# Merging the first transfers, reordering the rest, and moving one more pair of tiles from TensorE to VectorE

## Chip, cores, metric

One core of a Trainium2 chip. The metric is the device time of one execution in microseconds (us), taken as the median of several executions.

## The reference

```python
batch, m, k, n = 16, 512, 1024, 768          # float32 throughout
out = scale * matmul(x, weight) + add_value  # x: (16,512,1024), weight: (1024,768), scale = 0.1
```

The 8192 rows of x are worked off as 64 tiles of 128 rows. The bytes: x 33.55 MB, weight 3.15, add_value 25.17, output 25.17, together 87.03 MB.

## The kernel before

One list is the whole order of the transfers. `x`, `w`, `a` are loads of x tiles, weight chunks and add_value tiles, `o` (and `l`, `r` for the last tile's two pieces) are stores; the numbers are the first tile and how many. All are issued by one queue, in this order. The loop runs tile steps only as far as the next transfer needs them.

```python
STREAM = [
    ("x", 0, 3), ("w", 0, 2), ("w", 2, 2), ("w", 4, 2), ("x", 3, 1), ("w", 6, 2),
    ("a", 0, 3), ("x", 4, 4), ("a", 3, 1), ("x", 8, 4), ("a", 4, 4), ("x", 12, 4),
    ("a", 8, 8), ("x", 16, 8), ("a", 16, 8), ("x", 24, 8), ("a", 24, 8), ("o", 0, 8),
    # ... 20 more, ending in
    ("o", 56, 4), ("o", 60, 1), ("o", 61, 1), ("o", 62, 1), ("l", 63, 1), ("r", 63, 1),
]
X_SLOTS = 16    # tiles of x on the chip at a time
A_SLOTS = 32    # tiles of add_value; the result is written over them and stored from there
PAIRS = [14, 19, 24, 29, 34, 39, 44, 49, 54]   # tiles t, t+1 are turned by VectorE
```

A tile of x is cast to bf16 (GpSimd), turned so that its columns lie on partitions, multiplied, and evicted with scale and add_value (VectorE). Most tiles are turned by TensorE (four transposes into PSUM, then a copy by ScalarE); those in `PAIRS` by VectorE in four quarters, one after each eviction:

```python
def step():
    t = done["step"]
    # ... for the last tile: column pieces instead
    for j in range(KJ):                      # 8 chunks of the contraction
        if j == KJ // 2:
            if t + 1 not in in_pair:
                transpose(t + 1)             # TensorE
            cast_to(min(t + AHEAD, done["x"] - 1))
            if t + 7 in PAIRS:
                cast_pair(t + 7)             # GpSimd
        product(t, j, BOTH)                  # columns 0-511 and 512-767
    finish(t, BOTH[0], 0, N)                 # VectorE: scale, add, write over add_value
    for a in range(P // 32):
        if t + 6 - a in PAIRS:
            turn_pair(t + 6 - a, a)          # VectorE, a quarter of the pair
```

A partition holds eight neighbouring rows of x, add_value and output in memory (`(g p t) k -> p g t k`, t = 8), so an eight-tile x transfer is one 32 KB row for each partition, an add_value or output transfer one of 24 KB. The weight's rows come in runs of two, 6 KB.

## Time and profile before

| | kernel before |
|---|---|
| median time | 210.84 us (210.78 to 210.85, 3 runs) |
| TensorE busy | 196.4 us of a span of 209.2 |
| transfers, packets | 38, 5485 |
| moved | 87.03 MB by the kernel's queue, busy 97.7% |

The profile's busy rows show the share of each of 40 slices in tenths. The chain of waits is followed backwards from the last instruction. A trace also tells when each transfer's completion was counted, sixteen counts for a transfer, one for each DMA engine; "lands" below is the sixteenth, and "spread" is the sixteenth less the first. The lines that carry the reading are in the prediction. One more is needed for comparison, of the timeline of GpSimd: the cast that waits for x tiles 24 to 31.

```profile
73.31 2.03 POOL L109 CAST vx<-xs 128x1024 bf16<-128x1024 f32 x2 [9.08 <-DMA xs<-in_x_dram]
```

Columns: start, busy time, engine and line, what it does, how often, and in brackets the idle time before it and what ended it. These tiles landed at 73.17.

### The profile page before, as it was taken

What the parts mean: (1) busy time and instruction counts of PE and PEld (TensorE: products, weight loads), DVE (VectorE), ACT (ScalarE), POOL (GpSimd) and SP (SyncE); (2) the same over time, 40 slices, a digit from 0 to 9 for tenths busy, and PEclk for the clock granted to TensorE, in tenths of its full rate; (3) what the DMA queues carried; (4) which work ended last, traced back from release to release, by engine and by line L of the source; (5) the groups of instructions that cost most, each with busy time, mean ns of one, the idle gap of its engine ahead of it and who ended that gap; (6) DMA issues with size and microseconds to landing.
All of it is one profiled execution on the core that took longest, in us unless ns stands there. A gap on an engine that the chain in (4) does not pass through costs nothing.

```text
span 209.2 us, 2988 instructions
## 1 busy us (share of the span) xinstructions
PE 196.4 (94%) x1218; PEld 119.5 (57%) x1218; DVE 131.1 (63%) x223; ACT 49.3 (24%) x52; POOL 63.2 (30%) x69
## 2 busy tenths in 40 slices
PE   7599499999999999999999999999999999999990
PEld 2355256656665666566665666565666656666550
DVE  0545413309969969898697886949994994223340
ACT  2513113233103112113032031121130230332310
POOL 1310536420292090503903606303503039100000
PEclk9889979999999999999999999999999999999997
DMA  6999999999999999999999999999999999999993
GB/s 233 418 431 447 423 408 441 451 445 407 404 481 410 418 432 418 432 451 415 437 417 436 436 421 425 442 434 423 423 432 445 445 409 418 432 447 426 409 402 152
DMA packets 5485, 87.21 MB, mean 417 GB/s; under 512 B 608, under 2 KB 736, under 8 KB 2016
## 3 DMA queue, kind: packets, MB, share of 16 engines
q1 hardware_dynamic: 5472, 87.03, 97.7%
q8 instruction: 9, 0.15, 0.3%
q14 instruction: 4, 0.03, 0.0%
HBM read 61.87 MB, written 25.17 MB: 416 GB/s over the span
## 4 chain that ended last, share of the span: by engine, by line
PE 90%; DMA 3%; DVE 2%; ACT 1%; POOL 0%; issue 0%; ACTq 0%; POOLq 0%
PE mm L168 80%; PE tp L146 10%; DMA xs<-in_x_dram 3%; DVE ao L235 1%; ACT xt L152 1%; DVE ao L204 1%; POOL xb L136 0%; DVE xb L132 0%; DVE ao L176 0%; ACTq L152 0%; POOLq L136 0%
## 5 line engine op out<-in xcount | busy, mean ns | idle before, releaser
L168 PE MATMUL mm<-w_bf,xt 128*128 128x512 bf16 (+1 forms) x736 | 130.8, 331 | 0.6 <-DVE ao L204 0.4
L168 PEld LDWEIGHTS <-xt 128*128 128x128 bf16 x736 | 69.6, 99 | 50.8 <-ACT xt L152 11.4
L176 DVE SCALAR_TENSOR_TENSOR ao<-mm,ao 128x768 f32<-128x768 f32 (+2 forms) x62 | 58.3, 944 | 54.1 <-PE mm L168 35.3
L152 ACT COPY xt<-tp 128x1024 bf16<-128x1024 bf16 (+1 forms) x49 | 46.6, 961 | 146.0 <-PE tp L146 146.0
L120 DVE STREAM_TRANSPOSE vt<-vx 32x256 f32<-32x256 f32 x144 | 62.7, 435 | 6.2 <-POOL vx L109 4.0
L136 POOL CAST xb<-xs 128x1024 bf16<-128x1024 f32 x43 | 43.2, 1040 | 56.2 <-DMA xs<-in_x_dram 46.5
L168 PE MATMUL mm<-w_bf,vt 128*128 128x512 bf16 (+1 forms) x288 | 49.7, 326 | 0.0
L168 PEld LDWEIGHTS <-vt 128*128 128x128 bf16 x288 | 28.2, 98 | 17.5
L109 POOL CAST vx<-xs 128x1024 bf16<-128x1024 f32 x18 | 18.3, 1040 | 53.8 <-DVE vt L120 44.7
L146 PE MATMUL tp<-identity,xb 128*128 128x128 f32 x184 | 28.3, 277 | 5.4 <-POOL xb L136 3.0
L146 PEld LDWEIGHTS tp<-identity,xb 128*128 128x128 f32 x184 | 21.7, 143 | 12.1 <-POOL xb L136 3.4
L104 DVE CAST w_bf<-ao 128x768 bf16<-128x768 f32 x8 | 4.1, 557 | 3.8 <-DMA ao<-in_weight_dram 3.8
L132 DVE CAST xb<-xs 128x512 bf16<-128x512 f32 x3 | 1.9, 696 | 5.6 <-DMA xs<-in_x_dram 5.6
L94 PE MATMUL warm<-zeros 128*128 128x512 bf16 x10 | 4.3, 617 | 1.2 <-DVE zeros L82 1.2
L134 POOL CAST xb<-xs 128x512 bf16<-128x512 f32 x2 | 1.6, 834 | 5.5 <-DMA xs<-in_x_dram 5.5
L94 PEld LDWEIGHTS <-zeros 128*128 128x128 bf16 x10 | 1.3, 140 | 3.4 <-issue 2.2
L204 DVE TENSOR_SCALAR ao<-mm 128x768 f32<-128x768 f32 x2 | 1.8, 952 | 2.3 <-PE mm L168 2.3
L235 DVE TENSOR_TENSOR ao<-ao 128x768 f32<-128x768 f32 x3 | 2.7, 950 | 0.0
L134 ACT CAST xb<-xs 128x512 bf16<-128x512 f32 x1 | 0.6, 618 | 4.8 <-DMA xs<-in_x_dram 4.8
L134 ACT ACT_TABLE_LOAD x1 | 1.3, 1283 | 0.7 <-PEq L279 0.7
L201 ACT ACTIVATE ao<-mm 128x768 f32<-128x768 f32 x1 | 0.8, 817 | 0.0
L82 DVE MEMSET zeros<- 128x256 uint32 x1 | 0.3, 272 | 0.9 <-PEq L279 0.9
(6 smaller groups left out, 0.9 us busy)
## 6 DMA issues: line engine op xcount, KB each, us to landing
xs<-in_x_dram SPq DMA_DIRECT2D x6, 4096.0 KB, 27.3
ao<-in_add_value_dram SPq DMA_DIRECT2D x7, 3072.0 KB, 24.3
out_dram<-ao SPq DMA_DIRECT2D x7, 3072.0 KB, 31.2
xs<-in_x_dram SPq DMA_DIRECT2D x3, 2048.0 KB, 22.0
ao<-in_weight_dram SPq DMA_DIRECT2D x4, 768.0 KB, 9.5
xs<-in_x_dram SPq DMA_DIRECT2D x1, 1536.0 KB, 6.0
ao<-in_add_value_dram SPq DMA_DIRECT2D x1, 1536.0 KB, 23.7
out_dram<-ao SPq DMA_DIRECT2D x1, 1536.0 KB, 11.7
```

Of the source, the lines that this page charges most:

```text
L94: nc.tensor.matmul(warm[:, 0:CUT], zeros[:, 0:P], zeros, start=True, stop=True)
L104: nc.vector.tensor_copy(w_bf[:, j + i, :], ao[:, s + i, :])
L109: nc.gpsimd.tensor_copy(vx[:, i, :], xs[:, (t0 + i) % X_SLOTS, :])
L120: nc.vector.transpose(vt[b:b + 32, :, 32 * a:32 * a + 32], pairs[32 * a:32 * a + 32, :, b:b + 32])
L134: other(xb[:, K // 2:K], src[:, K // 2:K])
L136: nc.gpsimd.tensor_copy(xb, src)
L146: nc.tensor.transpose(tp[:, c, :], pairs[:, c * P:(c + 1) * P], identity)
L152: nc.scalar.copy(dst[:, c:c + q, :, :], src[:, c:c + q, :, :])
L168: nc.tensor.matmul(mm_tiles[t, cols[0]][:, n0:n1], lhs(t, j), w_bf[:, j, n0:n1], start=(j == 0), stop=(j == KJ - 1))
L176: nc.vector.scalar_tensor_tensor(a, mm_tiles[t, part][:, n0:n1], float(scale), a, op0=mybir.AluOpType.mult, op1=mybir.AluOpType.add)
L204: nc.vector.tensor_scalar(ao[:, EARLY_AT + t, :], mm_tiles[t, BOTH[0]][:, 0:N], float(scale), None, op0=mybir.AluOpType.mult)
L235: nc.vector.tensor_add(ao[:, t, :], ao[:, EARLY_AT + t, :], ao[:, t, :])
```

## The change

The intent: fewer and longer transfers at the start, where TensorE waits for data; loads and stores in an order that has add_value in time; less work for TensorE, the engine with the highest share.

```diff
 STREAM = [
-    ("x", 0, 3), ("w", 0, 2), ("w", 2, 2), ("w", 4, 2), ("x", 3, 1), ("w", 6, 2),
-    ("a", 0, 3), ("x", 4, 4), ("a", 3, 1), ("x", 8, 4), ("a", 4, 4), ("x", 12, 4),
-    ("a", 8, 8), ("x", 16, 8), ("a", 16, 8), ("x", 24, 8), ("a", 24, 8), ("o", 0, 8),
-    ("x", 32, 8), ("a", 32, 8), ("x", 40, 8), ("o", 8, 8), ("x", 48, 8), ("a", 40, 8),
-    ("o", 16, 8), ("o", 24, 8), ("a", 48, 8), ("x", 56, 8), ("a", 56, 8), ("o", 32, 8),
-    ("o", 40, 8), ("o", 48, 8), ("o", 56, 4), ("o", 60, 1), ("o", 61, 1), ("o", 62, 1),
-    ("l", 63, 1), ("r", 63, 1),
+    ("x", 0, 4), ("w", 0, 4), ("w", 4, 4), ("a", 0, 4), ("x", 4, 4), ("x", 8, 4),
+    ("a", 4, 4), ("x", 12, 4), ("a", 8, 8), ("x", 16, 8), ("a", 16, 8), ("x", 24, 8),
+    ("o", 0, 8), ("a", 24, 8), ("x", 32, 8), ("a", 32, 8), ("x", 40, 8), ("o", 8, 8),
+    ("o", 16, 8), ("a", 40, 8), ("x", 48, 8), ("a", 48, 8), ("x", 56, 8), ("o", 24, 8),
+    ("o", 32, 8), ("a", 56, 8), ("o", 40, 8), ("o", 48, 8), ("o", 56, 4), ("o", 60, 2),
+    ("o", 62, 1), ("l", 63, 1), ("r", 63, 1),
 ]
-PAIRS = [14, 19, 24, 29, 34, 39, 44, 49, 54]
+PAIRS = [14, 19, 24, 29, 34, 39, 44, 49, 54, 59]
-    w_v = weight.rearrange("(c p r) n -> p c r n", p=P, r=2)
+    w_v = weight.rearrange("(c p r) n -> p c (r n)", p=P, r=2)
     # load_w: one transfer now takes n chunks (four), in runs of two rows
+        nc.sync.dma_start(
+            ao[:, s:s + n, :].rearrange("p (c r) n -> p c (r n)", r=2),
+            w_v[:, j // 2:(j + n) // 2, :])
     # [cut: the old load_w, and the head's test for the first x transfer]
```

More of the change, by code (lines that the diff above doesn't have):

```diff
@@ L98, in load_w @@
         s = A_SLOTS - KJ + j
-        if n == 1:
-            nc.sync.dma_start(ao[:, s, :], w_v[:, j // 2, j % 2, :])
-        else:
-            nc.sync.dma_start(ao[:, s:s + 2, :], w_v[:, j // 2, :, :])
+        assert j % 2 == n % 2 == 0
+        nc.sync.dma_start(
+            ao[:, s:s + n, :].rearrange("p (c r) n -> p c (r n)", r=2),
+            w_v[:, j // 2:(j + n) // 2, :])
         for i in range(n):
@@ L249 @@
             done["x"] = s + n
-            if last < EARLY:
+            if s < EARLY:
                 head(op, s, n)
```

## The prediction

> **What bounds the kernel now.** I read the page first, for which engines are full; then the chain of waits, for what the end hangs on; then the timeline of the issuing queue, for which transfer waits for whom; then windows at the end, for who is last.
>
> ```profile
> PE 196.4 (94%) x1218; PEld 119.5 (57%) x1218; DVE 131.1 (63%) x223; ACT 49.3 (24%) x52; POOL 63.2 (30%) x69
> DMA  6999999999999999999999999999999999999993
> q1 hardware_dynamic: 5472, 87.03, 97.7%
> PE 90%; DMA 3%; DVE 2%; ACT 1%; POOL 0%; issue 0%; ACTq 0%; POOLq 0%
> ```
>
> Two resources are full at once. TensorE has 94% and carries 90% of the chain, but the transfers are busy in every slice from the second to the last but one. Stretches of the chain:
>
> ```profile
> 20.67 2.61 DVE ao L235 x3
> 24.36 0.66 PE tp L146 x4
> 25.01 4.28 PE mm L168 x16
> 29.29 0.44 PE tp L146 x4
> 29.73 2.63 PE mm L168 x16
> 203.61 0.42 DVE ao L176
> ```
>
> A tile costs TensorE 2.63 us of products, plus 0.44 if TensorE also turns it. From 24.36 (tile 4's turning) to 203.6 TensorE never stops for more than a fraction. The 4.28 in place of 2.63 is a half-clock stretch (25.8 to 29.2) after an idle of 3.04 us. Before 24.36 it waits for x: tiles 4 to 7 land at 23.21, as the timeline shows by GpSimd's cast:
>
> ```profile
> 6.77 0.33 SPq L254 DMA_DIRECT2D ao<-in_add_value_dram  x1
> 8.61 0.33 SPq L248 DMA_DIRECT2D xs<-in_x_dram  x1
> 23.26 3.99 POOL L136 CAST xb<-xs 128x1024 bf16<-128x1024 f32 x4 [8.52 <-DMA xs<-in_x_dram]
> 138.85 0.96 DVE L176 SCALAR_TENSOR_TENSOR ao<-mm,ao 128x768 f32<-128x768 f32 x1 [3.08 <-DMA ao<-in_add_value_dram]
> 160.82 0.96 DVE L176 SCALAR_TENSOR_TENSOR ao<-mm,ao 128x768 f32<-128x768 f32 x1 [3.06 <-DMA ao<-in_add_value_dram]
> ```
>
> Row one shows that eight transfers can be in flight: the ninth issue comes just after the first landing (6.75). Windows at the end (columns: PE, PEld, DVE, ACT, POOL busy, clock, DMA share, GB/s):
>
> ```profile
> 203.00:204.00 1.00, 0.57 (x6) 0.27 (x3) 0.82 (x2) 0.00 (x0) 0.00 (x0) 1.00 0.96 384
> 204.00:205.00 1.00, 0.00 (x0) 0.00 (x0) 0.04 (x1) 0.00 (x0) 0.00 (x0) 1.00 0.94 373
> 205.00:206.00 1.00, 0.00 (x0) 0.00 (x0) 0.00 (x0) 0.00 (x0) 0.00 (x0) 1.00 0.78 293
> 206.00:207.00 1.00, 0.00 (x0) 0.00 (x0) 0.00 (x0) 0.00 (x0) 0.00 (x0) 0.83 0.26 94
> ```
>
> TensorE and VectorE are done, yet the DMA engines are still 0.94 and 0.78 busy: stores were queued. The trace's completion records say it sharper. The last store was issued at 204.06; the first of the 16 engines finished it at 205.66 (1.6 us, an unqueued store), the slowest at 208.20 (4.1 us). The last tiles' stores, issued at 195.82, 198.89 and 201.96, land at 205.40, 206.31 and 207.24, 0.92 us apart: 0.393 MB at the queue's full rate, not the 3.07 us apart at which TensorE makes tiles. So the end is set by the slowest DMA engine, and TensorE has about 4.1 - 1.6 = 2.5 us of room although the chain names it. The slowest engine is late because each of nine 16 KB instruction loads (every 20 us) takes one engine 1.0 to 1.5 us; the load at 189.9 puts one engine 1.3 us behind all others.
>
> **What the Trainium skill says.** "DMA: Bandwidth & Descriptors", section "Where 436 GB/s comes from", gives 435 GB/s as the ceiling of the fabric; here a 4.19 MB load lands 9.70 us after the one ahead, 432 GB/s, so there is no rate left to gain. Same page, "Queues, rings and completion order": an engine takes its descriptors in ring order. All landings here come in order of issue, so a transfer's landing is told by the bytes issued up to and with it. Same page, "Why a DMA increments its semaphore by 16 and not by 1": only the full 16 says that all has landed; here the 16 spread from 0.3 us early to 2.5 us at the end. "TensorE: Matmul & The Clock Gate", section "What's actually happening": the clock falls to half after an idle window of 3413 ns, windows running free; the trace has two half-clock records of 3.41 us (8.7 to 12.1, 25.8 to 29.2).
>
> **The change part by part.**
>
> Bytes: the same 87.03 MB. Packets of the weight stay 6 KB (the four rows are two runs).
>
> Fewer transfers: 33 for 38. Landing intervals give the fixed cost of one: 0.786 MB of weight take 1.88 us against 0.786 / 0.432 = 1.82; the 0.524 MB tile 1.28 against 1.21. So 0.06 us each, five fewer save 0.3 us of queue time, and this is on the path, since the queue is full to the end.
>
> Head, by bytes and landings of before. x 0-3: 2.10 MB, 6.75 + 0.524/0.42 = 8.0 (was 6.75 for three tiles). First weight half: 3.67 MB, 11.7. Second: 5.24 MB, 15.4. x 4-7 now follow all four add_value rows, 8.91 MB, where before landed 24.18; less about 0.2 for four fewer transfers, 24.0. So tile 4 starts 0.8 us later: TensorE +0.8. The first products move from 10.05 to about 12.3 (11.7 plus a cast of 0.56), but 24 groups of two matmuls at 0.33 us, 7.9 us, end at about 20.5, and tile 3's first half at about 22.4, before tile 4 can begin at 25.1. That delay lies in the existing wait. TensorE's idle before tile 4 is about 2.8 us instead of 3.0: the half-clock window (1.65 us) may come or not.
>
> Pair 59/60: TensorE loses two turnings, 2 x 0.44 = 0.88 us, ScalarE 2 x 1.01. VectorE gains 16 transposes x 0.435 = 7.0 us between 175 and 188, where it is idle 2.1 us of each 3.07. GpSimd's two casts of 1.04 only change target. Net for TensorE: +0.8 - 0.88, about zero; its end stays near 203.6.
>
> Stream order, followed by hand with the landing at a given sum of bytes (63.5 us at 25.17 MB, then 0.432 MB per us). A transfer leaves when its slot is free and those ahead have left. x 24-31 leave at 43.3 (casts of tiles 14, 15), as before. a 32-39 need the first store's landing, 32.51 MB, 80.5 (was 87.8). x 40-47 leave at about 88.7, while the queue is filled to 104.7. a 40-47 need the second store, 50.33 MB, 121.7, filled to 129. x 48-55 follow at 122, filled to 136. a 48-55 leave at 129 (filled to 146), x 56-63 at about 132 (to 153). a 56-63 need store 24-31, 71.30 MB, 170.3, filled to 177.6. So the queue is never empty; the shortest lead is about 7 us.
>
> Who waits for the moved loads: a 40-47 land at 136.3 instead of 138.8 and a 48-55 at 153.3 instead of 160.7, so the two VectorE waits shown go. x 48-55 land at 146.0 instead of 131.4: pair 49 is cast by 149.1 (was 146.6), and its four turnings, each 1.78 with a 0.96 eviction between, end at about 159.4; TensorE wants it at about 160. a 56-63 land at 184.8 instead of 177.7: tile 56's eviction slips from 182.6 to 184.9, and the last quarter of pair 59 ends at 187.7, wanted at about 189. Both fit by 1 us or so, and a slip of up to 2.5 us would not reach the end.
>
> Sum: 0.3 us less of queue, everything else beside it: 210.84 - 0.3 = 210.5 us.
>
> **The rivals.** (a) TensorE is the bound, as its chain says: then later x 4-7 (+0.8), the pair (-0.88) and the clock window (-1.65 to +1.65) decide, 209.1 to 212.4. For it: 90% of the chain. Against: stores landing at the queue's rate after TensorE's end. It can bind only if it loses over 2 us. (b) A late load becomes the wait: x 48-55 or a 56-63 stall pair 49 or 59, some 1 to 2 us of TensorE; with the clock window also lost, the end moves by perhaps 0.5 to 1 us: 211 to 211.5. For it: margins of about 1 us; against: the 2.5 us of room. (c) The lag of the slowest engine changes: the load of instructions at 189.9 falls on another engine, 1.3 us less (209.2), or a second one is hit twice, 1 us more (211.5). Sixteen fewer TensorE instructions among 2436 should not shift the pattern. (d) The head's larger transfers fill the queue sooner (its rate is 86 and 184 GB/s in the second and third us): at most a few tenths, 210.2.
>
> **Range and chances.** 2% is 4.2 us. Faster by that would need the queue to move 87 MB above 440 GB/s; slower, an empty queue of 4 us, which the replay does not find but may have missed in one of its waits. Rival (c) is the widest on both sides. Predicted 210.5 us, range 209.7 to 211.4; faster 0.01, same 0.97, slower 0.02.
>
> **What would show it.** Right: DMA at 9 in all middle slices; last stores landing about 0.9 us apart per tile and more than 3 us after issue on the slowest engine; TensorE's last product within 1.7 us of 203.5; x 4-7 cast at about 24 instead of 23.26; GpSimd waiting for x near 146; VectorE's waits for add_value gone near 138 and 160, a new one near 184.8. Wrong: a slice of the DMA row under 9 in the middle, the last store landing 1.6 to 2 us after its issue (then TensorE was the bound), or TensorE idle before tiles 49 or 59 for over 2 us.

## The result

211.13 us (210.87 to 211.39, 6 runs) against 210.82 (210.56 to 210.93, 6 runs) for the kernel before in the same rounds: ratio 1.0017, 95% interval 1.0004 to 1.003. A ratio is the mean time of one kernel's fast runs over that of the other's of the same rounds, so it is not quite the ratio of the medians. The time is inside the predicted range and within 2%, but on the other side of the kernel before: 0.3 us longer, where 0.3 us less was predicted.

The page after, the rows that answer to those of before:

```profile
PE 195.5 (93%) x1210; PEld 118.4 (57%) x1210; DVE 139.5 (67%) x239; ACT 47.3 (23%) x50; POOL 65.0 (31%) x69
DMA  7999999999999999999999999999999999999993
DMA packets 5021, 87.21 MB, mean 417 GB/s; under 512 B 528, under 2 KB 656, under 8 KB 1552
q1 hardware_dynamic: 5008, 87.03, 97.7%
DMA 58%; PE 21%; DVE 10%; POOL 4%; issue 2%; SPq 2%; POOLq 0%
```

The work of the engines moved as planned: TensorE and ScalarE have less, VectorE 8.4 us more. The transfers are as full as before. Yet the chain of waits, which was 90% TensorE, is now 58% DMA, for a time that differs by 0.17%. Part of it:

```profile
122.82 23.75 DMA xs<-in_x_dram
...
147.67 2.04 POOL vx L108 x2
149.73 0.43 DVE vt L119
...
159.45 0.45 DVE vt L119
159.90 0.05 issue
159.95 4.08 PE mm L167 x24
```

It runs through x tiles 48 to 55 and the turning of pair 49, for which TensorE waited 0.92 us, as the timeline confirms. The same timeline has the other places that the prediction named:

```profile
24.30 8.63 POOL L135 CAST xb<-xs 128x1024 bf16<-128x1024 f32 x7 [13.30 <-DMA xs<-in_x_dram]
73.97 2.02 POOL L108 CAST vx<-xs 128x1024 bf16<-128x1024 f32 x2 [9.77 <-DMA xs<-in_x_dram]
136.94 0.96 DVE L175 SCALAR_TENSOR_TENSOR ao<-mm,ao 128x768 f32<-128x768 f32 x1 [1.55 <-DMA ao<-in_add_value_dram]
159.95 1.37 PE L167 MATMUL mm<-w_bf,vt 128*128 128x512 bf16 x7 [0.92 <-DVE vt L119]
185.60 0.96 DVE L175 SCALAR_TENSOR_TENSOR ao<-mm,ao 128x768 f32<-128x768 f32 x1 [2.62 <-DMA ao<-in_add_value_dram]
```

Row two was not foreseen: x 24-31 land at 73.82, 0.65 us later than before, though the same bytes are issued up to and with them in both orders (29.36 MB). The windows at the end have the shape they had before:

```profile
203.00:204.00 1.00, 0.36 (x4) 0.07 (x1) 0.64 (x2) 0.00 (x0) 0.00 (x0) 1.00 0.86 353
204.00:205.00 1.00, 0.00 (x0) 0.00 (x0) 0.00 (x0) 0.00 (x0) 0.00 (x0) 1.00 0.95 374
205.00:206.00 1.00, 0.00 (x0) 0.00 (x0) 0.00 (x0) 0.00 (x0) 0.00 (x0) 1.00 0.69 264
```

The last store was issued at 203.84 (before 204.06); the first engine finished it at 205.46 and the slowest at 208.34 (before 205.66 and 208.20). TensorE was 0.2 us earlier, the slowest engine 0.14 us later. So of the 0.65 us at 73.82 only 0.14 are left at the end of these two profiles.

### The profile page after: what moved, and what is told of

It reads as the page before. It is cut to its first block, busy times and chain, and to the rows that moved or that the text cites. A ratio compares the mean times of both kernels' runs of the same rounds, so it can differ in the third digit from the quotient of the medians.

```text
span 209.3 us, 2975 instructions
## 1 busy us (share of the span) xinstructions
PE 195.5 (93%) x1210; PEld 118.4 (57%) x1210; DVE 139.5 (67%) x239; ACT 47.3 (23%) x50; POOL 65.0 (31%) x69
## 4 chain that ended last, share of the span: by engine, by line
DMA 58%; PE 21%; DVE 10%; POOL 4%; issue 2%; SPq 2%; POOLq 0%
DMA xs<-in_x_dram 43%; PE mm L167 19%; DMA out_dram<-ao 16%; DVE vt L119 7%; POOL vx L108 4%; DVE ao L175 3%; PE tp L145 2%; SPq L253 1%; SPq L247 1%; POOL xb L135 1%; SPq L99 0%; POOLq L135 0%; POOLq L108 0%
## 5 line engine op out<-in xcount | busy, mean ns | idle before, releaser
L167 PE MATMUL mm<-w_bf,xt 128*128 128x512 bf16 (+1 forms) x704 | 124.2, 329 | 1.3 <-DVE w_bf L103 0.8
L167 PEld LDWEIGHTS <-xt 128*128 128x128 bf16 x704 | 66.2, 99 | 49.5 <-ACT xt L151 10.9
L151 ACT COPY xt<-tp 128x1024 bf16<-128x1024 bf16 (+1 forms) x47 | 44.7, 958 | 146.3 <-PE tp L145 146.3
L119 DVE STREAM_TRANSPOSE vt<-vx 32x256 f32<-32x256 f32 x160 | 69.7, 436 | 12.1 <-POOL vx L108 9.5
L167 PE MATMUL mm<-w_bf,vt 128*128 128x512 bf16 x320 | 55.3, 326 | 0.9 <-DVE vt L119 0.9
L167 PEld LDWEIGHTS <-vt 128*128 128x128 bf16 x320 | 31.2, 98 | 20.7 <-DVE vt L119 1.3
L108 POOL CAST vx<-xs 128x1024 bf16<-128x1024 f32 x20 | 20.3, 1041 | 47.2 <-DVE vt L119 36.5
L145 PE MATMUL tp<-identity,xb 128*128 128x128 f32 x176 | 27.6, 281 | 4.4 <-DVE xb L131 3.1
L145 PEld LDWEIGHTS tp<-identity,xb 128*128 128x128 f32 x176 | 21.0, 144 | 11.0 <-issue 4.0
L234 DVE TENSOR_TENSOR ao<-ao 128x768 f32<-128x768 f32 x3 | 4.4, 1507 | 0.0
```

The source lines that it names most:

```text
L108: nc.gpsimd.tensor_copy(vx[:, i, :], xs[:, (t0 + i) % X_SLOTS, :])
L119: nc.vector.transpose(vt[b:b + 32, :, 32 * a:32 * a + 32], pairs[32 * a:32 * a + 32, :, b:b + 32])
L145: nc.tensor.transpose(tp[:, c, :], pairs[:, c * P:(c + 1) * P], identity)
L151: nc.scalar.copy(dst[:, c:c + q, :, :], src[:, c:c + q, :, :])
L167: nc.tensor.matmul(mm_tiles[t, cols[0]][:, n0:n1], lhs(t, j), w_bf[:, j, n0:n1], start=(j == 0), stop=(j == KJ - 1))
L234: nc.vector.tensor_add(ao[:, t, :], ao[:, EARLY_AT + t, :], ao[:, t, :])
```

## The experiments

Two questions. Is it the transfer queue (theory Q) or TensorE (theory T) that sets the end? And where are the predicted 0.3 us, and 0.3 us more? All timed runs were compared with the kernel before on the same chip and in the same rounds; the other runs were not all timed together. A median is that of 4 to 6 executions (split: 2). By the rule of 2%, only split differs from the kernel before (slower); differences of 0.1 to 0.2% are read from the intervals, and are near the noise.

| run | what it is | median us | ratio, 95% interval | TensorE's last product, last landing (profile) |
|---|---|---|---|---|
| before | | 210.8 | 1 | 203.57, 208.20 |
| after | all of the change | 211.13 | 1.0017 (1.0004 to 1.0030) | 203.36, 208.34 |
| pair_only | before + pair 59 | 210.79 | 1.0002 (0.9990 to 1.0015) | 202.29, 208.02 |
| no_pair | after - pair 59 | 211.16 | 1.0018 (1.0006 to 1.0031) | 204.34, 208.79 |
| pe_plus2 | after + 2 us of matmuls | 211.15 | 1.0023 (1.0011 to 1.0036) | 205.01, 208.42 |
| pe_plus5 | after + 4.9 us of matmuls | 213.28 | 1.0131 (1.0100 to 1.0162) | 208.31, 210.58 |
| no_load | after - 3.15 MB (wrong result) | 207.38 | 0.9833 (0.9820 to 0.9846) | 202.36, 204.63 |
| no_load_no_pair | the same - pair 59 | 208.08 | 0.9860 (0.9842 to 0.9877) | 203.80, 206.07 |
| head_only | before, merged head | 210.87 | 1.0005 (0.9992 to 1.0019) | 203.17, 208.08 |
| after_swapped | after, one exchange undone | 210.81 | 0.9996 (0.9983 to 1.0008) | 202.73, 208.07 |
| before_swapped | before, that exchange done | 211.15 | 1.0012 (0.9999 to 1.0024) | 203.33, 208.30 |
| old_head | after, head of before | 211.04 | 1.0014 (1.0002 to 1.0027) | 203.11, 208.37 |
| w_rows | after_swapped, longer weight rows | 211.20 | 1.0011 (0.9997 to 1.0026) | 203.51, 208.64 |
| split | before, two x loads cut up | 221.60 | 1.0505 (1.0485 to 1.0525) | 214.30, 218.52 |

### The pair alone

```diff
-PAIRS = [14, 19, 24, 29, 34, 39, 44, 49, 54]          # in the kernel before
+PAIRS = [14, 19, 24, 29, 34, 39, 44, 49, 54, 59]
```

> The kernel before with pair 59/60 added and nothing else. Theory Q (the full transfer queue, through its slowest DMA engine, sets the end): no gain, within 0.3 us of before (ratio 0.9985 to 1.0015), although TensorE's last product comes 0.9 us earlier (about 202.7 instead of 203.6). Theory T (TensorE sets the end): 0.9 us faster, ratio 0.996.

TensorE's last product came 1.3 us earlier (0.9 expected; the half-clock stretch before tile 4 is missing in this run too, so not all of it is the pair's) and the time did not move. In the windows at the end the engines stop in the 203rd us, and the queue goes on as in the kernel before:

```profile
202.00:203.00 1.00, 0.29 (x3) 0.01 (x1) 0.57 (x2) 0.00 (x0) 0.00 (x0) 1.00 0.95 387
203.00:204.00 1.00, 0.00 (x0) 0.00 (x0) 0.00 (x0) 0.00 (x0) 0.00 (x0) 1.00 1.03 412
204.00:205.00 1.00, 0.00 (x0) 0.00 (x0) 0.00 (x0) 0.00 (x0) 0.00 (x0) 1.00 0.92 362
205.00:206.00 1.00, 0.00 (x0) 0.00 (x0) 0.00 (x0) 0.00 (x0) 0.00 (x0) 1.00 0.67 258
```

Theory T falls here: 1.3 us off the engine that fills 90% of the chain bought nothing.

### The change without the pair

The same line the other way, in the changed kernel.

> The changed kernel without pair 59/60: the new stream alone. Theory Q: as the changed kernel, within 0.3 us of it (about 211.1, ratio to before 1.000 to 1.003), with TensorE's last product 0.9 us later, near 204.3. Theory T: 0.9 us slower than the changed kernel, 212.0, ratio 1.006.

The ratio is that of the whole change. So the 0.3 us come from the order or the head, not from the pair or from VectorE's added work.

### More work for TensorE

```diff
         if t < T - 1:
+            if t == 60:
+                for _ in range(6):          # 15 in the second run
+                    product(t, 0, BOTH, whole=True)   # a closed group, written again by the real one
             for j in range(KJ):
```

> The changed kernel with 12 more matmuls (six repeats of tile 60's first group, 6 x 0.33 = 2.0 us) on TensorE, result unchanged. Theory Q: TensorE ends 2.0 us later (205.4), the last store is issued at 205.8 instead of 203.8, and the end moves by 0.0 to 0.5 us (ratio to before 1.0015 to 1.004), because the slowest engine was busy until 208.3. Theory T: 2.0 us slower, ratio 1.011.

> The changed kernel with 30 more matmuls (15 x 0.33 = 4.9 us) on TensorE. Theory Q: TensorE's room of some 2.9 us (last store issued at 203.8, slowest engine 208.3, an unqueued store 1.6) is used up; the last store is issued at about 208.7 and lands at about 210.4, so the end moves by 2.0 us, not 4.9: ratio to before about 1.011. Theory T: 4.9 us, ratio 1.025.

With 2 us more the time stayed (211.15; the changed kernel 211.13 in other rounds). With 4.9 us more it rose by 213.28 - 211.13 = 2.15. The room is therefore about 4.9 - 2.15 = 2.8 us (2.5 if the two ratios are compared instead of the medians), where the prediction had 2.5 and the expectation 2.9. In the second run the queue runs empty between the last stores, which it does neither before nor after the change:

```profile
206.00:207.00 1.00, 1.00 (x6) 0.47 (x5) 0.67 (x1) 0.00 (x0) 0.00 (x0) 1.00 0.40 139
207.00:208.00 1.00, 1.00 (x10) 0.76 (x8) 0.53 (x1) 0.00 (x0) 0.00 (x0) 1.00 0.47 181
208.00:209.00 1.00, 0.30 (x3) 0.02 (x1) 0.59 (x2) 0.00 (x0) 0.00 (x0) 1.00 0.54 212
209.00:210.00 1.00, 0.00 (x0) 0.00 (x0) 0.00 (x0) 0.00 (x0) 0.00 (x0) 1.00 0.98 354
```

DMA shares of 0.40 and 0.47 under a busy TensorE are here the picture of a kernel that TensorE ends; 0.94 and 0.95 in the first full us without TensorE (204 to 205), as before and after, that of one which the queue ends. Here the last store landed 1.78 us after its issue, against 4.1 and 4.5 in those two.

### Less work for the queue

```diff
-    ("o", 16, 8), ("a", 40, 8), ("x", 48, 8), ("a", 48, 8), ...
+    ("o", 16, 8), ("x", 48, 8), ("a", 48, 8), ...     # rows 40-47 are wrong on purpose
```

> The changed kernel without the load of add_value rows 40-47 (3.15 MB, 7.3 us of queue; wrong result on purpose for those rows). Theory Q: the queue stops being the bound, the last stores leave unqueued and land 1.6 us after issue on all engines, 205.4 instead of 208.3, if TensorE still ends near 203.4: 2.5 to 3 us faster, ratio to before 0.988. Theory T: no change, ratio 1.0015.

> As the run without the load of add_value rows 40-47 (wrong on purpose), and without pair 59/60 too. Theory Q: with the queue relieved TensorE is the bound, so here the pair's 2 x 0.44 us do count: 0.9 us slower than the run with the pair (207.4), 208.2 to 208.3, ratio to before 0.988. If the pair were of no use to TensorE at all: 207.4 again.

Without 3.15 MB the time fell by 3.75 us from 211.13. That is more than the 2.5 to 3 expected, because TensorE itself ended 1.0 us earlier. The queue now runs empty between the last stores, as it did with 4.9 us more work for TensorE:

```profile
200.00:201.00 1.00, 1.00 (x6) 0.49 (x5) 0.72 (x1) 0.00 (x0) 0.00 (x0) 1.00 0.37 141
201.00:202.00 1.00, 1.00 (x10) 0.70 (x8) 0.47 (x1) 0.00 (x0) 0.00 (x0) 1.00 0.43 172
```

And now the pair pays: 208.08 - 207.38 = 0.7 us, where 0.9 was expected. The two runs were timed in different rounds; by their ratios it is 0.6 us, and the intervals just overlap. The pair, which is worth nothing in the full kernel, is worth most of its arithmetic once the queue is out of the way.

### The head alone

```diff
-    ("x", 0, 3), ("w", 0, 2), ("w", 2, 2), ("w", 4, 2), ("x", 3, 1), ("w", 6, 2),
-    ("a", 0, 3), ("x", 4, 4), ("a", 3, 1), ("x", 8, 4), ...
+    ("x", 0, 4), ("w", 0, 4), ("w", 4, 4), ("a", 0, 4), ("x", 4, 4), ("x", 8, 4), ...
```

> The kernel before with the merged head alone (first five transfers as after), the rest of the order, the pairs and the tail as before. Prediction's cost of 0.06 us for each transfer: tiles 4 to 7 land 0.2 us earlier than by bytes, near 24.0, and the end 0.2 us earlier. Rival (what was merged into larger rows saves 0.1 us each, but the larger first transfer starts slower and gives it back): tiles 4 to 7 land at 24.2 to 24.3 as in the changed kernel, and the time is within 0.2 us of before.

The rival holds: the first 8.91 MB landed at 24.25 (before 24.18), not at 24.0. Over all profiles but one (w_rows, whose weight rows differ) the old head gives 24.18 to 24.29 (five kernels) and the merged one 24.03 to 24.28 (eight). Four transfers fewer saved nothing that shows. The landings say why. The weight took 3.76 + 3.76 us in two transfers (3.74 + 3.77 in the changed kernel), 1.84 + 1.89 + 1.88 + 1.87 in four: the same, 7.5. And the first 2.10 MB landed at 8.13 here, at 8.15 in the changed kernel, no sooner than 6.75 + 1.28 = 8.03, which is three tiles and one tile of before one after the other.

### One exchange in the order

The late landing at 73.82 in the result asks what differs there. In the changed order the first store of the kernel follows x 24-31 directly; before, add_value 24-31 lay between.

```diff
-    ("x", 24, 8), ("o", 0, 8), ("a", 24, 8),          # changed kernel
+    ("x", 24, 8), ("a", 24, 8), ("o", 0, 8),          # after_swapped; before_swapped is the reverse
```

> The changed kernel with one exchange in its order: the load of add_value rows 24-31 goes ahead of the first store (0-7) again, as in the kernel before. Theory S (the first store right behind the 32 KB rows of x slows the last of those rows on the engines that lag, near 70 us): x 24-31 land at 73.1 to 73.3 instead of 73.8, the burst of slow packets near 70 us is gone, the end comes 0.3 to 0.5 us earlier than in the changed kernel, ratio to before 0.999 to 1.000. Rival H (the head with its 16 KB rows costs it): x 24-31 still at 73.8 and ratio 1.002.

> The kernel before with the opposite exchange: the first store ahead of add_value rows 24-31. Theory S: x 24-31 land near 73.7 instead of 73.2 and the time is 0.3 to 0.5 us longer, ratio 1.0015 to 1.0025. Rival H: no change, ratio 1.000.

With the exchange undone the cast of pair 24 starts as early as in the kernel before:

```profile
73.12 2.02 POOL L108 CAST vx<-xs 128x1024 bf16<-128x1024 f32 x2 [9.15 <-DMA xs<-in_x_dram]
```

x 24-31 landed at 72.98 instead of 73.82, and the time is that of the kernel before, 210.81. The packets in the trace show what happens near 69.5 to 70.8 in the changed kernel. A 32 KB row takes an engine 1.22 us; eight rows that start between 69.5 and 70.8 take 0.1 to 0.8 us longer, and the spread of the sixteen engines grows from 1.95 to 2.56 us. It stays so: 2.56 two stores later. The first row of the store starts at 70.92. Five of the slow rows started by 69.72 and ended between 70.9 and 71.2, so they were slow mostly before any row of the store is on record.

The opposite exchange in the kernel before cost somewhat less time than expected, 1.0012, an interval that just touches 1; but its profile has only three slow rows there, x 24-31 at 73.39, and hardly any growth of the spread (1.91 to 1.94).

### The head of before under the new order

```diff
-    ("x", 0, 4), ("w", 0, 4), ("w", 4, 4), ("a", 0, 4), ("x", 4, 4), ("x", 8, 4),
+    ("x", 0, 3), ("w", 0, 2), ("w", 2, 2), ("w", 4, 2), ("x", 3, 1), ("w", 6, 2),
+    ("a", 0, 3), ("x", 4, 4), ("a", 3, 1), ("x", 8, 4),   # the rest as in the changed kernel
```

> The changed kernel with the head of before (nine transfers up to tile 7's rows, then the new order, the pair and the merged tail). Theory S (the order alone makes the burst of slow rows at the first store): x 24-31 land some 0.6 us late as in the changed kernel, the spread of the 16 engines grows there from about 1.8 to 2.4, ratio to before 1.0015 to 1.0025. Theory B (the burst needs the merged head too, as the small burst in the kernel before with the exchange hints): the spread grows by under 0.15 us, ratio 1.000 to 1.001.

```profile
73.72 2.02 POOL L109 CAST vx<-xs 128x1024 bf16<-128x1024 f32 x2 [9.58 <-DMA xs<-in_x_dram]
```

Theory S: x 24-31 landed at 73.57 and the spread grew from 1.69 to 2.19, with the old head too; ratio 1.0014. The merged head is not needed. Over all fourteen profiles, with the store directly behind x 24-31 these land at 73.39 to 73.90 (eight kernels, the two without the load among them); with add_value between, at 72.98 to 73.30 (six). The growth of the spread shows how clean that line is: 0.40 to 0.65 us in seven of the eight, 0.03 in before_swapped; 0.06 and less in five of the six, 0.27 in split, where the one slow row (69.94) follows an instruction load at 68.87.

Two things in the same traces limit the reading. Up to store 8-15, old_head and before_swapped issue the same transfers in the same order, yet the spread grew by 0.50 us in one and 0.03 in the other: the order allows the burst, but does not alone decide its size. And the later stores that directly follow eight-tile loads of x show nothing of the kind: in the changed kernel the spread went from 2.53 to 2.51 at x 40-47 and from 2.51 to 2.49 at x 56-63; over all runs it grew at such places by at most 0.19. So what the runs show belongs to the first store, not to any store behind a long load.

### Are longer rows or fewer transfers cheaper?

```diff
+            if s == 32:                                  # same rows, four transfers
+                for p in range(0, P, 32):
+                    nc.sync.dma_start(xs[p:p + 32, k:k + n, :], src[p:p + 32])
+            elif s == 48:                                # rows of 8 KB, four transfers
+                for i in range(0, n, 2):
+                    nc.sync.dma_start(xs[:, k + i:k + i + 2, :], src[:, i:i + 2, :])
```

> The kernel before with x 32-39 loaded as four transfers of 32 partitions (three transfers more, rows as long as before) and x 48-55 as four transfers of two tiles (three transfers more, four times as many rows, 8 KB each, 24 rows more for each engine). Prediction's cost by transfer (0.06 us each): both groups land 0.2 us later after the transfer ahead than the 9.66 and 9.66 us of before. Rival, cost by row (0.0115 us for each row on each engine): the first group unchanged at 9.7, the second 0.28 us longer, 9.9 to 10.0.

The second half answers: the four transfers of 8 KB rows landed 2.48, 2.50, 2.48 and 2.48 us apart, 9.94 in all against 9.66 before. That is 0.28 us for 24 rows more, 0.0117 a row, and more than three transfers at 0.06 would make. The first half failed as an experiment. A transfer of only 32 partitions ran at half rate, so the cost of a transfer as such could not be read. Each 1.05 MB took 4.9 to 5.1 us, and the windows (GB/s last) show the DMA engines busy and slow:

```profile
88.00:108.00 20.00, 19.90 (x127) 12.43 (x128) 12.63 (x22) 3.97 (x4) 0.82 (x1) 1.00 0.93 203
```

"SBUF — State Buffer", section "Door 1: The DMA port swizzle (why `[64,N]` ≈ `[32,N]`)", would have told: bandwidth goes by how many of the 16 ports the partitions reach, and by its formula 32 partitions in a row reach eight. The 203 GB/s agree. I had not looked it up for this experiment.

### A candidate to beat both

```diff
-    w_v = weight.rearrange("(c p r) n -> p c (r n)", p=P, r=2)
+    w_v = weight.rearrange("(p j) n -> p j n", p=P)      # a partition's eight rows are neighbours
-                nc.gpsimd.tensor_copy(xb, src)
+                nc.gpsimd.tensor_copy(to, src)           # casts deal x's columns to chunks likewise
```

> A candidate to beat both: the changed kernel with add_value 24-31 ahead of the first store, and the columns of x dealt to chunks so that a partition's weight rows are neighbours: 12 KB rows instead of 6 KB, 16 rows less for each engine. Cost by row: 16 x 0.0115 = 0.18 us less, each weight half lands 0.09 us sooner, ratio to the kernel before 0.998 to 1.000 (210.4 to 210.8). Cost by transfer: as without it, 0.9996. Either way the casts read with strides and may be slower, which stays beside the path unless GpSimd's cast grows by over a half.

The weight halves landed 3.66 and 3.68 us apart instead of 3.74 and 3.77: 0.085 us for eight rows less, 0.011 a row, as the cost by row says. But the time is 211.2: in this profile the burst of slow rows came too, now at the end of add_value 24-31 (77.2), where the first store follows; that load took 7.84 us instead of 7.3, and the spread grew from 2.02 to 2.48. After_swapped has a small burst at the same place (eight rows of 1.05 to 1.29 us instead of 0.91, spread 1.75 to 1.91). So add_value ahead of the store makes the burst rarer or smaller, not impossible. No correct version tried here is clearly faster than the kernel before.

## Why the prediction was right, and where not

- **The queue sets the end, through its slowest engine.** Right, and shown both ways: 1.3 us off TensorE and 2 us onto it left the time alone, 3.15 MB off the queue took 3.75 us.
- **TensorE has about 2.5 us of room.** Right: 2.5 to 2.8 by the run with 4.9 us of matmuls more.
- **The pair is worth 0.88 us to TensorE and nothing to the time.** Right: 0.6 to 0.7 us once the queue was relieved, none before.
- **Five transfers fewer save 0.06 us each, 0.3 us.** This step failed. The intervals it was worked out from (1.88 against 1.82) do show a cost, but it goes with the rows of the loads, about 0.011 us for each row on each engine. The two weight halves have as many rows as the four quarters, and they took the same 7.5 us. By rows the head should still have gained 16 x 0.011 = 0.18 us from the joined x and add_value rows; the first transfer with its longer rows landed 0.1 us late and the rest of the gain is too small to see. The last joined store landed 1.83 us behind, against 0.93 + 0.91 for two. It too has eight rows fewer on each engine and gained 0.01 us, not 0.09: the cost by row was measured on loads and does not hold for these stores.
- **The order costs nothing, since the queue never runs empty.** It never did: every issue came within 1 us of the times followed by hand (121.7 became 122.4, 170.3 became 170.9), and the landings within 0.7. But "full" is not "at the same rate": with the first store directly behind the 32 KB rows, the last rows on the engines that lagged were slower, 0.6 us on the slowest. This is the likeliest cost behind the 0.3 us: with the exchange undone the ratio fell from 1.0017 to 0.9996, which is just more than the noise. How much of it reaches the end differs from run to run. In the profile of the changed kernel the instruction load near 188 left the latest engine 3.64 us behind the first and the next one 2.72, which is where the engine that the burst had put last stood (2.66): another one ended last. At that load the spread grew by 0.98 us, before the change by 1.31. This is rival (c), the changed lag of the slowest engine, in a small measure; no rival named the burst. That the burst goes with this exchange is shown in the new order, by seven profiles with it and two without (one of these, w_rows, has its burst one load later); in the order of before it was hardly there. Why rows of a load slow down there, why only at the first store, and what brought the burst to the other order in one run, is not shown.
- **The head delays TensorE by 0.8 us.** Partly. The x tiles 4-7 landed at 24.25 (24.0), tile 4's turning began at 25.63 (25.1), 1.27 us later than before: GpSimd's casts took 1.25 us on average instead of 1.04 (the slowest 1.76), and VectorE's three adds beside them 1.51 instead of 0.95. TensorE's idle before tile 4 was 1.17 us, not 2.8, since the first products ended at 24.46, not at 22.4. The half-clock stretch there did not come, which gave back 1.65. Together: +1.27 - 1.65 - 0.88 for the pair + 0.92 for pair 49's wait = -0.3 us; TensorE ended 0.2 us earlier. That its end stayed near 203.6 is in part luck.
- **The clock falls to half after an idle window of 3413 ns** (cited in the prediction). The length is in the trace. But before the change the window ahead of the half-clock stretch, 22.35 to 25.76, was not an idle one: TensorE worked in it from 24.36 on.
- **Pairs 49 and 59 fit by 1 us or so.** Nearly: pair 49's last quarter ended at 159.9 (predicted 159.4) and TensorE waited 0.92 us for it, since the half-clock window before tile 4 did not come and TensorE was earlier. The room swallowed it. Tile 56's eviction came at 185.6 (184.9), pair 59 in time.
- **VectorE's waits near 138 and 160 go.** Half: the second went, the first shrank from 3.08 to 1.55 us.
- **A gain of 2% needs more than 440 GB/s.** The sum is a little off: from the first landing (2.10 MB at 8.0) to an end at 204.0, 84.9 MB in 196 us are 433 GB/s. It is still above the 432 that the queue showed.

## What to carry to other kernels

When two resources are both full, the chain of waits may name either one (here 90% TensorE before, 58% DMA after, at the same time). Look at the last stores instead: if they land at the queue's own pace, long after their issue, work taken from the engines buys nothing, and adding a little work to the engine tells how much room it has. What counted in this full queue was the number of rows in its loads and how far behind the slowest engine was; a smaller count of transfers gave nothing. And the place of the first store among the loads was worth about half a microsecond on the lagging engines, that of later stores at most 0.2; try such an exchange both ways round.

## What the Trainium skill lacked or had wrong

- "DMA: Bandwidth & Descriptors", section "Queues, rings and completion order", knows row 14 as runtime-internal; what instruction loads cost a full transfer queue is not told there. Here nine loads of 16 KB (on queue 8) and four of 8 KB (on queue 14) ran beside the kernel's queue, each of the nine about 1.0 to 1.1 us long; the sixteen engines, 0.4 and 0.6 us apart at the first landing (before and after the change), ended 2.5 and 2.9 us apart.
- The same page, "Rules for kernel authors", asks for 1 MiB or more in a transfer for full bandwidth. Behind other transfers in a full queue that did not matter: stores of 0.39 MB landed 0.92 us apart, 0.43 MB/us, the rate of 4 MB transfers. For loads, what counted was 0.011 us for each row on each engine.
- No page has the burst at the first store: rows of 1.22 us took up to 2.0, the spread of the engines grew by 0.4 to 0.65 us in seven profiles.
